# One group of square sums, an earlier modulation column and sooner expected landings in a planned layer kernel

## The chip, the cores and the metric

The kernel runs on one core of a Trainium2 chip, in one launch. The metric is the device time in microseconds of that core. A core has a tensor engine (TensorE, PE in the profile) that multiplies matrices out of SBUF into PSUM, a vector engine (VectorE, DVE), a scalar engine (ScalarE, ACT), a general engine (GpSimd, POOL) and a queue engine (SyncE, SP) that here issues nearly all DMA loads. Each engine takes its instructions strictly in the order in which the program gives them.

## The reference

One layer over 512 latent tokens and 256 context tokens of width 1024, in float32. The part that the change is about is the opening: the modulation from c, the normalisation of x, and the first projection.

```python
def rms_norm(x, w):
    y = xf * lax.rsqrt(jnp.mean(xf * xf, axis=-1, keepdims=True) + EPS)
    return (y * w.astype(jnp.float32)).astype(x.dtype)

def modulate(h, shift, scale):
    return h * (1 + scale) + shift
...
mod_x = jnp.split((jax.nn.silu(c) @ w_mod[l] + b_mod[l])[:, None, :], N_MOD, axis=-1)
mod_c = jnp.split((jax.nn.silu(c_ctx) @ w_mod[l] + b_mod[l])[None, None, :], N_MOD, axis=-1)
cq_x, ckv_x, kr_x, z_x, xbc_x, dt_x = in_split(
    modulate(rms_norm(x, mix_pre_norm[l]), mod_x[0], mod_x[1]) @ w_in[l])
```

After it come latent attention over 16 heads, a bidirectional state-space scan over 16 heads (whose output is multiplied by silu(z)), one output projection, a normalised residual, and a gated MLP of inner width 2816 with a convolution of width 3 on the gate.

## The kernel before

x lies transposed: 8 blocks of 128 features by 512 tokens. Wide products run as three passes of 32-bit reduced precision on split operands (a rounded part and the rest, made by ScalarE at L500 and VectorE at L501).

**Opening.** The 8 blocks of x are loaded first (L492), then small parameters, then the weights block by block. ScalarE squares each block (L611, in `token_scale`). VectorE adds squares (L613); the argument `firsts` names the blocks at which a new group of adds starts. When a group ends, four products with a column of ones (L619, two instructions each) add it over the features into one bank. With groups at 0, 2, 4 and 6 there are four adds and 16 products. Then VectorE takes mean and inverse root (L623, L522 to L531), four products (L537) spread the result as a row, and ScalarE copies it (L630).

The modulation of a block needs two dot products of silu(c) with columns k and 8+k of `w_mod`. For blocks 2, 4 and 6 (`ON_PE`) TensorE does them (`moddots`, L599: eight products for a column, 16 instructions); for the others VectorE does (`moddot`, L589), with c spread over all partitions by `spread` (L664, L666). `modulated` (L635 to L645) applies scale and shift. Then 12 products of 512 columns (`half_of_z`, L687) add block k to the first half of z. Blocks go in the order 0, 2, 1, 4, 3, 6, 5, 7. The second half of z and the later projections follow.

Filler products on zeros (L680, 128 x 128 times 128 x 256) stand in three lots whose sizes are `IDLE`. The first must come before the spread of c, the second after it, the third after the products of the square sums.

**The planner.** The order on each engine is not the order of the source. `plan` prices each instruction, builds the dependences, and `Graph.schedule` lists them by rank, forward and backward, over 24 rounds, together with the place of each buffer in SBUF; the round with the shortest planned time is kept. Loads marked `urgent` keep the order of the source. `pins` are added dependences between products: each pair of instructions in one stretch must precede all of another. The second column of block 2 is pinned behind the z products of block 0, its first behind L537; the columns of blocks 4 and 6 behind z products of blocks before theirs. Filler that has no pin ahead of it is put wherever the plan has TensorE idle.

A load is planned as: issue, a start of 650 ns, a transfer at 360 bytes per ns behind all loads planned before it in the queue, and then a wait of 910 ns plus 0.8 of its transfer before its readers may start. At most eight loads are planned in flight. The planner also models TensorE's rate: it halves the rate in a tick of 3413 ns when too little was streamed in the tick before.

Of the kernel before, what the change touches and what calls it, by code (L numbers as in the profile page):

```python
# [20 lines left out]
S = 512  # L21
CT = 256
T = S + CT
KD = D // P
# [57 lines left out]

ON_PE = 2, 4, 6
BLOCKS = 0, 2, 1, 4, 3, 6, 5, 7
IDLE = 22, 13, 13
PACE = 1.25


# [24 lines left out]
class Banks:  # L113
# [18 lines left out]
    def put(self, *aps):  # L132
        for ap in aps:
# [6 lines left out]
WAITS = {("Activation", "Activation"): 75, ("Activation", "DVE"): 142, ("Activation", "PE"): 271, ("Activation", "Pool"): 170,  # L140
         ("DVE", "Activation"): 128, ("DVE", "DVE"): 127, ("DVE", "PE"): 256, ("DVE", "Pool"): 155,
         ("PE", "Activation"): 197, ("PE", "DVE"): 196, ("PE", "Pool"): 224,
         ("Pool", "Activation"): 75, ("Pool", "DVE"): 74, ("Pool", "PE"): 149, ("Pool", "Pool"): 102}

AHEAD = 40000
DMA_START, DMA_WAIT, DMA_AHEAD, DMA_ALONE, RUN, FLYING = 650, 910, 3000, 0.8, 80, 8


def engine_of(x):
# [113 lines left out]
class Graph:  # L263
# [16 lines left out]
    def wait(self, i, j):  # L280
        if self.back:
            i, j = j, i
        return DMA_WAIT + DMA_ALONE * self.cost[i] if self.dma[i] else WAITS.get((self.eng[i], self.eng[j]), 0)

    def reversed(self):
        g = Graph.__new__(Graph)
# [25 lines left out]
    def schedule(self, rank, look=0.06):  # L312

        n = len(self.preds)
        left, ready = [len(p) for p in self.preds], [0.0] * n
        start, end = [0.0] * n, [0.0] * n
        later, now = {e: [] for e in ENGINES}, {e: [] for e in ENGINES}
        clock, order, queue = {e: 0.0 if self.back else BEGIN for e in ENGINES}, {e: [] for e in ENGINES}, 0.0
        ticks, held, port, flying = {}, 0, 0.0, []
        for i in range(n):  # L320
            if not left[i]:
                ready[i] = max(0.0, rank[i] - AHEAD) if i in self.opens else 0.0
                heapq.heappush(later[self.eng[i]], (ready[i], rank[i], i))

        def open_until(e, t):
            while later[e] and later[e][0][0] <= t:
                _, r, i = heapq.heappop(later[e])
                heapq.heappush(now[e], (r, i))

        for _ in range(n):  # L330
            while True:
                at = []
                for e in ENGINES:
                    open_until(e, clock[e])
                    if now[e] or later[e]:
                        at.append((clock[e] if now[e] else later[e][0][0], e))
                t, e = min(at, key=lambda v: v[0])
                open_until(e, t)
                r, i = heapq.heappop(now[e])
                sooner = [v for v in later[e] if v[1] < r and v[0] < t + (look if v[1] > r - 5000 else 0.8) * self.cost[i]]  # L340
                if not sooner:
                    break
                heapq.heappush(now[e], (r, i))
                clock[e] = min(sooner, key=lambda v: v[1])[0]
            order[e].append(i)
            if self.tables[i] not in (None, held):
                held, t = self.tables[i], t + TABLE
            if self.shared[i]:
                t = max(t, port)
                port = t + self.cost[i]  # L350
            if self.dma[i] and not self.back and len(flying) >= FLYING:
                t = max(t, flying[-FLYING])
            start[i] = t
            end[i] = t + self.cost[i] if self.back or e != "PE" else self.product(t, i, ticks)
            clock[e] = end[i] + (3 if e == "PE" else 0)
            if self.dma[i] and e != "SP":
                end[i], clock[e] = max(t + self.dma[i] + DMA_START + 600, queue) + self.cost[i], t + 60
                queue += self.cost[i]
            if e == "SP":
                end[i] = queue = max(t + self.dma[i] + DMA_START, queue) + self.cost[i]  # L360
                clock[e] = t + self.dma[i] if self.back else max(t + self.dma[i], queue - DMA_AHEAD)
            if self.dma[i]:
                flying.append(end[i] + DMA_WAIT + DMA_ALONE * self.cost[i])
            for j in self.succs[i]:
                ready[j] = max(ready[j], end[i] + self.wait(i, j))
                left[j] -= 1
                if not left[j]:
                    if j in self.opens:
                        ready[j] = max(ready[j], rank[j] - AHEAD)
                    heapq.heappush(later[self.eng[j]], (ready[j], rank[j], j))  # L370
        return max(end), order, start, end
# [97 lines left out]
def build(nc, tc, ctx, a, out, dbg=None, places=None):  # L469
    mm = nc.tensor.matmul  # L470
    act = nc.scalar.activation
    V, G = nc.vector, nc.gpsimd
# [10 lines left out]
    def t4(*shape, dt=F32):  # L483
        return sl.get(here(), shape or (P, 1024), dt)

    def t2(*shape, dt=F32):
        return sl.get(here(), shape or (P, 512), dt)
# [26 lines left out]
    def small(tag, w=1):  # L514
        cnt[0] += w
        return smalls[:, cnt[0] - w : cnt[0]]
# [17 lines left out]
    def rows_of(po, r, n):  # L534

        for i in range(n):
            mm(po[:, i * P : (i + 1) * P], lhsT=r[:, i : i + 1].to_broadcast([P, P]), rhs=ident, start=True, stop=True)  # L537
# [10 lines left out]
    xt = [t4(P, 2, S) for _ in range(4)]  # L548
# [17 lines left out]
    def R(name, j=0, n=1):  # L566
        o, w = PRM[name]
        return prm[:, o + j : o + j + n]
# [22 lines left out]
    def moddots(k, w0, w1, pm):  # L591

        for n, w in enumerate((w0, w1)):
            began = here()
            at = BLOCKS.index(k) - 3 + n
            o = products[BLOCKS[max(at, 0)]] if at > -2 else rows
            pins.extend(((o[0] + i, o[0] + i + 2), (began, began + KD)) for i in range(0, o[1] - o[0], 2))
            for r in range(KD):
                mm(pm[:, 2 * n : 2 * n + 2], lhsT=w[:, r * P : (r + 1) * P], rhs=cc[:, 2 * r : 2 * r + 2], start=r == 0,  # L599
                   stop=r == KD - 1)  # L600
        for n, md in enumerate((mod, modc)):
            V.tensor_tensor(out=md[:, k:16:8], in0=pm[:, n:4:2], in1=R("bmod", k, 9)[:, 0:9:8], op=ALU.add)

    def token_scale(blocks, n, firsts, kind):


        nt = n // P
        pS, began = pget(kind), here()
        for i, b in enumerate(blocks):
            sq = t2()  # L610
            act(sq if len(b.shape) == 2 else sq.rearrange("p (a b) -> p a b", a=2), b, AF.Square)  # L611
            if i not in firsts:
                firsts[j].tensor_tensor(out=part, in0=part, in1=sq, op=ALU.add)  # L613
            else:
                part, j = sq, i
            if i + 1 in firsts or i + 1 == len(blocks):
                for o in range(0, S, n):
                    for c in range(nt):
                        mm(pS[:, c : c + 1], lhsT=part[:, o + c * P : o + (c + 1) * P], rhs=ones[:, :1],  # L619
                           start=j == o == c == 0, stop=(i + 1 == len(blocks) and o + n == S and c == nt - 1))  # L620
        summed = began, here()
        ss = small(f"ss{nt}", nt)
        V.tensor_scalar(out=ss, in0=pS[:, :nt], scalar1=1.0 / D, scalar2=EPS, op0=ALU.mult, op1=ALU.add)  # L623
        pfree(pS)
        pr = pget(kind)
        r, began = rsqrt(ss, nt), here()
        rows_of(pr, r, nt)
        rows = began, here()
        rB = t2(P, n)
        act(rB, pr[:, :n], AF.Copy)  # L630
        return rB, pr, summed, rows
# [23 lines left out]
    act(cch, cc, AF.Tanh, scale=0.5)  # L655
    V.scalar_tensor_tensor(out=cc, in0=cch, scalar=1.0, in1=cc, op0=ALU.add, op1=ALU.mult)
    V.tensor_scalar(out=cc, in0=cc, scalar1=0.5, scalar2=None, op0=ALU.mult)
    rB, pr, summed, rows = token_scale([xt[k // 2][:, k % 2, :] for k in range(KD)], S, {0: V, 2: V, 4: V, 6: V}, "b")


    def spread(i, v):
# [14 lines left out]

    for i, n in enumerate(IDLE):
        began = here()
# [18 lines left out]
    kept, products, pmod = {}, {}, pget("m")  # L697
    hx.extend([None] * KD)
    for k in BLOCKS:
# [15 lines left out]
        began = here()  # L715
# [174 lines left out]
    pr = pget("b")  # L890
# [529 lines left out]
    rows = {}  # L1420
# [300 lines left out]
```

## Time and profile before

| what | us |
|---|---|
| median of 3 runs (lowest to highest) | 966.89 (965.46 to 972.02) |
| the profiled execution's own time | 967.49 |
| its span, first to last instruction | 965.7 |
| mean granted TensorE clock in it | 0.987 |
| DMA packets' bytes in it | 137.53 MB, 142 GB/s on average |

The profile is of one execution. A page names lines as L and a number, engines by the short names above, PEld for TensorE's weight loads. Rows of the windows view give a stretch of the span, then busy time and instruction counts of engines, the granted TensorE clock as a share of full speed, the mean busy share of the DMA engines, and GB/s. Rows of the chain view give start, length, and what the time is put down to, on the chain of work that ended last. Rows of the timeline give start, length, engine, line, operation, what it writes and reads, and in brackets how long the engine was idle before and what released it. Rows of the waits view give who waited for whom: total, times, longest.

### The profile page before, as it was taken

To read this page: it belongs to the slowest core of one execution; us is meant where nothing else is said; L and a number is where in the kernel's file an instruction comes from. 1 tells how busy PE (TensorE), PEld (TensorE's weight loads), DVE (VectorE), ACT (ScalarE), POOL (GpSimd) and SP (SyncE) were. 2 spreads that over 40 slices of the span, in tenths; PEclk is the share of its full clock that TensorE was granted. 3 is DMA by queue.
4 is the path that set the end of the run, shared out by engine and by line. 5 is a ranking of instruction groups with operands and counts; after the bars stand their busy time and mean duration, and the time that the engine had idled before them with its cause. 6 is when DMAs were issued, how large, how long until landed. Compare 5 with 4: busy or idle time off the path is not lost.

```text
span 965.7 us, 14674 instructions
## 1 busy us (share of the span) xinstructions
PE 944.0 (98%) x5118; PEld 805.6 (83%) x5118; DVE 763.3 (79%) x1452; ACT 525.7 (54%) x1024; POOL 236.5 (24%) x246
## 2 busy tenths in 40 slices
PE   9999999999999999999999999999999999999995
PEld 9888888888788888888988888988888888887784
DVE  5799868789979999987999967943556442799998
ACT  4364336635677787778886215732324322257782
POOL 0001000547768546734010100000011042230021
PEclk6999999999999999999999999999999999999998
DMA  9943111102331441545678764523255132346883
GB/s 345 338 162 107 31 52 66 50 12 83 94 79 50 102 116 40 135 106 132 180 236 290 266 212 172 207 80 131 69 186 190 58 106 90 123 143 199 257 277 127
DMA packets 54586, 137.53 MB, mean 142 GB/s; under 512 B 8032, under 2 KB 11120, under 8 KB 54512
## 3 DMA queue, kind: packets, MB, share of 16 engines
q1 hardware_dynamic: 53712, 134.92, 43.1%
q10 hardware_dynamic: 800, 1.68, 0.5%
q8 instruction: 40, 0.66, 0.3%
q14 instruction: 34, 0.28, 0.1%
HBM read 114.50 MB, written 6.34 MB: 125 GB/s over the span
## 4 chain that ended last, share of the span: by engine, by line
PE 81%; DVE 12%; DMA 3%; ACT 2%; issue 1%; POOL 0%; SPq 0%; DVEq 0%; ACTq 0%; POOLq 0%
PE banks L755 40%; PE banks L1319 7%; PE banks L1189 6%; PE banks L1551 5%; PE banks L687 5%; DVE block L501 5%; PE banks L1217 4%; PE banks L1205 4%; DVE block L1544 2%; PE banks L1023 1%; PE banks L599 1%; PE banks L1069 1%; PE banks L1124 1%; PE banks L1061 1%; DMA block<-in_wdn_dram 1%
## 5 line engine op out<-in xcount | busy, mean ns | idle before, releaser
L755 PE MATMUL banks<-block,block 128*128 128x512 f32 (+1 forms) x2132 | 450.6, 361 | 1.8 <-DVE block L1415 0.8
L755 PEld LDWEIGHTS banks<-block,block 128*128 128x128 f32 x2132 | 358.1, 188 | 63.3 <-issue 1.1
L500 ACT ACTIVATE block<-block 128x512 fp32r<-128x512 f32 (+4 forms) x340 | 216.2, 663 | 154.1 <-PE banks L755 28.0
L501 DVE TENSOR_TENSOR block<-block,block 128x512 fp32r<-128x512 f32 (+3 forms) x316 | 245.0, 810 | 33.9 <-PE banks L755 16.4
L1551 PE MATMUL banks<-block,block 128*128 128x512 f32 x462 | 108.7, 391 | 1.0 <-DVE block L501 0.8
L1551 PEld LDWEIGHTS banks<-block,block 128*128 128x128 f32 x462 | 86.0, 188 | 21.6 <-DVE block L501 3.2
L1189 PE MATMUL banks<-block,block 128*128 128x256 f32 (+1 forms) x384 | 93.5, 351 | 2.8 <-DMA block<-block 1.6
L501 DVE TENSOR_TENSOR block<-banks,block 128x256 fp32r<-128x256 f32 (+1 forms) x156 | 83.5, 555 | 10.6 <-ACT block L500 10.1
L1319 PE MATMUL banks<-block,block 128*128 128x512 f32 x384 | 89.3, 391 | 0.0
L1319 PEld LDWEIGHTS banks<-block,block 128*128 128x128 f32 x384 | 71.6, 188 | 14.6 <-DVE block L501 0.2
L500 ACT ACTIVATE block<-banks 128x256 fp32r<-128x256 f32 (+1 forms) x156 | 72.3, 495 | 15.1 <-PE banks L1205 10.0
L1189 PEld LDWEIGHTS banks<-block,block 128*128 128x128 f32 x384 | 59.5, 189 | 9.8 <-ACT block L1193 3.0
L1191 DVE TENSOR_REDUCE smalls<-banks 128x1 f32<-128x768 f32 x64 | 60.8, 950 | 8.1 <-PE banks L1189 6.4
L1217 PE MATMUL banks<-block,block 128*128 128x256 f32 x384 | 66.2, 294 | 0.2 <-ACT block L1193 0.2
L1193 ACT ACTIVATE block<-banks,smalls 128x768 f32<-128x768 f32 x64 | 57.6, 901 | 15.0 <-DVE smalls L1191 13.3
L1205 PE MATMUL banks<-cst,block 128*128 128x128 f32 x384 | 64.4, 273 | 0.5 <-DVE block L501 0.3
L589 DVE SCALAR_TENSOR_TENSOR block<-block,block 128x1024 f32<-128x1024 f32 x52 | 62.4, 1216 | 1.8 <-DMA block<-in_wmod_dram 1.8
L1446 ACT ACTIVATE block<-banks,prm 128x512 f32<-128x512 f32 x22 | 16.9, 775 | 84.7 <-PE banks L755 84.7
L785 DVE SCALAR_TENSOR_TENSOR block<-banks,cwh,block 128x510 f32<-128x510 f32 (+3 forms) x88 | 51.6, 622 | 11.7 <-ACT block L781 11.1
L1217 PEld LDWEIGHTS banks<-block,block 128*128 128x128 f32 x384 | 54.7, 189 | 3.5 <-ACT block L1193 0.4
L1460 POOL TENSOR_TENSOR block<-block 128x256 f32<-128x256 f32 x11 | 12.5, 1132 | 169.2 <-PE banks L755 69.6
L1205 PEld LDWEIGHTS banks<-cst,block 128*128 128x128 f32 x384 | 46.7, 141 | 7.6 <-DVE block L501 1.7
(230 smaller groups left out, 1120.5 us busy)
## 6 DMA issues: line engine op xcount, KB each, us to landing
block<-in_wdn_dram SPq DMA_DIRECT2D x99, 256.0 KB
block<-in_wmod_dram SPq DMA_DIRECT2D x48, 512.0 KB
block<-in_wup_dram SPq DMA_DIRECT2D x44, 512.0 KB
block<-block SPq DMA_DIRECT2D x32, 256.0 KB
block<-in_wout_dram SPq DMA_DIRECT2D x16, 512.0 KB
block<-in_wxbc_dram SPq DMA_DIRECT2D x12, 512.0 KB
block<-block SPq DMA_DIRECT2D x40, 128.0 KB
block<-in_wz_dram SPq DMA_DIRECT2D x16, 256.0 KB
```

Of the source, the lines that this page charges most:

```text
L500: act(hi, src, AF.Copy)
L501: (lo_eng or V).tensor_tensor(out=lo, in0=src, in1=hi, op=ALU.subtract)
L589: V.scalar_tensor_tensor(out=junk, in0=wt, scalar=0.5, in1=vec, op0=ALU.mult, op1=ALU.mult, accum_out=acc)
L755: mm(po, lhsT=wf(k, pt[0]), rhs=xf(k, pt[1]), start=(k == 0 and pt == parts[0]), stop=(k == nk - 1 and pt == parts[-1]))
L785: V.scalar_tensor_tensor(out=st[:, lo:hi], in0=pm[:, lo + d : hi + d], scalar=cwh[:, m * 5 + j : m * 5 + j + 1], in1=st[:, lo:hi], op0=ALU ...
L1189: mm(sc[:, o : o + n], lhsT=q_[:, x_, qi * P : (qi + 1) * P], rhs=kk[:, y_, :], start=part == 0, stop=part == 2)
L1191: V.reduce_max(nm, sc[:, :T], axis=AX.X, negate=True)
L1193: act(pe, sc[:, :T], AF.Exp, bias=nm, scale=1.0, accum_out=sum_)
L1205: nc.tensor.transpose((tx if c < NX else tc_)[:, o : o + P], pe[:, s_ : s_ + P], ident)
L1217: mm(po[:, half * 256 : half * 256 + 256], lhsT=vst(c), rhs=rhs, start=(part == 0 and c == 0), stop=(part == 1 and c == NKT - 1))
L1319: mm(po[i][:, nh * 512 : nh * 512 + 512], lhsT=l[lp][:, i * P : (i + 1) * P], rhs=w[wp][:, nh * 512 : nh * 512 + 512], start=(k == 0 and l ...
L1551: mm(po[i], lhsT=l[:, lp, i * P : (i + 1) * P], rhs=w[wp], start=first and q == 0 and n == 0, stop=q == PAIRS[-1] and n == 2, skip_group_c ...
```

## The change

Four edits, in the order of the diff. The three lots of filler grow from 22, 13, 13 to 22, 44, 24. The planner's landing time changes: a load's data is now there at the later of its own undisturbed landing (start, 1.8 of its transfer) and the planned end of the queue less 600 ns, plus 910 ns; loads issued by engines other than SP now also start no earlier in the queue than their own start. This enters the forward plan, the backward plan and the count of loads in flight, so all orders and buffer places may come out differently. The second modulation column of block 2 is pinned behind the row products (L537) and no longer behind block 0's z products. The squares of x form one group: seven adds on VectorE, then four products.

```diff
-IDLE = 22, 13, 13
+IDLE = 22, 44, 24
...
-DMA_START, DMA_WAIT, DMA_AHEAD, DMA_ALONE, RUN, FLYING = 650, 910, 3000, 0.8, 80, 8
+DMA_START, DMA_WAIT, DMA_AHEAD, DMA_ALONE, RUN, FLYING, DMA_FULL = 650, 910, 3000, 0.8, 80, 8, 600
...
-        return DMA_WAIT + DMA_ALONE * self.cost[i] if self.dma[i] else WAITS.get((self.eng[i], self.eng[j]), 0)
+        return DMA_WAIT if self.dma[i] else WAITS.get((self.eng[i], self.eng[j]), 0)
...
             if self.dma[i] and e != "SP":
-                end[i], clock[e] = max(t + self.dma[i] + DMA_START + 600, queue) + self.cost[i], t + 60
-                queue += self.cost[i]
+                began = t + self.dma[i] + DMA_START + 600
+                queue = max(began, queue) + self.cost[i]
+                end[i], clock[e] = max(began + (1 + DMA_ALONE) * self.cost[i], queue - DMA_FULL), t + 60
             if e == "SP":
-                end[i] = queue = max(t + self.dma[i] + DMA_START, queue) + self.cost[i]
+                began = t + self.dma[i] + DMA_START
+                queue = max(began, queue) + self.cost[i]
+                end[i] = max(began + (1 + DMA_ALONE) * self.cost[i], queue - DMA_FULL)
                 clock[e] = t + self.dma[i] if self.back else max(t + self.dma[i], queue - DMA_AHEAD)
             if self.dma[i]:
-                flying.append(end[i] + DMA_WAIT + DMA_ALONE * self.cost[i])
+                flying.append(end[i] + DMA_WAIT)
...
             at = BLOCKS.index(k) - 3 + n
-            o = products[BLOCKS[max(at, 0)]] if at > -2 else rows
+            o = products[BLOCKS[at]] if at >= 0 else rows
...
-    rB, pr, summed, rows = token_scale([xt[k // 2][:, k % 2, :] for k in range(KD)], S, {0: V, 2: V, 4: V, 6: V}, "b")
+    rB, pr, summed, rows = token_scale([xt[k // 2][:, k % 2, :] for k in range(KD)], S, {0: V}, "b")
```

## The prediction

> **What bounds the kernel now.** I read the page's head first, then the busy time by stretches of the span, then the chain that ended last through the opening, and last the VectorE and ScalarE timelines of the same microseconds.
>
> ```profile
> span 965.7 us, 14674 instructions
> PE 944.0 (98%) x5118; PEld 805.6 (83%) x5118; DVE 763.3 (79%) x1452; ACT 525.7 (54%) x1024; POOL 236.5 (24%) x246
> PE 81%; DVE 12%; DMA 3%; ACT 2%; issue 1%; POOL 0%; SPq 0%; DVEq 0%; ACTq 0%; POOLq 0%
> ...
> 0.00:25.00 25.00, 23.27 (x113) 22.43 (x114) 13.34 (x40) 10.98 (x19) 0.80 (x7) 0.68 0.94 346
> 25.00:50.00 25.00, 25.00 (x151) 22.14 (x150) 18.94 (x42) 10.98 (x20) 0.00 (x0) 0.98 0.91 341
> 250.00:275.00 25.00, 22.05 (x134) 18.74 (x133) 22.53 (x43) 18.76 (x47) 15.37 (x16) 1.00 0.38 96
> 950.00:965.70 15.70, 4.51 (x20) 3.38 (x19) 11.58 (x49) 2.10 (x6) 1.29 (x1) 0.75 0.36 134
> ```
>
> TensorE is busy for 944.0 of 965.7 us, and the chain lies on it for 81%. So time is won only where TensorE does nothing, does filler, or runs slowly. Idle time is 21.7 us in all: 1.7 in the first 25 us, 11.2 in the tail after 950, and 8.8 spread between (the largest piece 2.95, in the stretch from 250). In the row from 25 to 50 there is none: products fill every gap. A product stream that starts its useful work earlier therefore ends earlier, as long as data is there. The granted clock (third number from the right) is 0.68 only in the first stretch. The opening is where the change's named parts lie:
>
> ```profile
> 1.20:5.65 4.45, 4.41 (x20) 1.00 0.83 252
> 5.65:9.06 3.41, 2.92 (x27) 1.00 1.05 367
> 9.06:12.47 3.41, 3.41 (x17) 0.50 1.01 389
> 12.47:15.89 3.42, 3.42 (x18) 0.50 1.04 416
> 19.30:22.71 3.41, 3.41 (x17) 0.50 1.04 405
> 22.71:26.13 3.42, 3.42 (x10) 0.50 0.97 327
> 26.13:29.54 3.41, 3.41 (x27) 1.00 0.98 389
> ...
> 7.75 0.50 PE banks L664 x4
> 8.25 0.84 PE banks L619 x8
> 10.28 1.79 PE banks L619 x8
> 12.49 1.50 PE banks L619 x8
> 13.99 2.77 PE banks L680 x12
> 16.76 1.81 PE banks L537 x8
> 18.57 3.21 PE banks L599 x16
> 21.77 1.27 PE banks L680 x5
> 23.05 4.25 PE banks L687 x12
> 27.29 1.68 PE banks L599 x16
> 28.97 0.71 PE banks L680 x5
> 31.36 2.87 PE banks L687 x12
> ```
>
> The first seven rows (TensorE alone: stretch, busy, products, granted clock, DMA share, GB/s) show the clock at half from 9.06 to 26.13 us, five steps of 3.41. The rest is the chain: L664 the spread of c over partitions, L619 the sums of squares, L680 filler, L537 the row of scales, L599 a modulation column, L687 z products. At half clock twelve z products take 4.25 us against 2.87 later, a column 3.21 against 1.68, eight sum products 1.79 against 0.84. The first block's z products end at 27.29, and only then comes block 2's second column (27.29) and filler (28.97). At 29.68 the next column starts; this is my yardstick, T.
>
> **The change, part by part.**
>
> ```profile
> 8.21 2.60 ACT L611 ACTIVATE block<-block 128x512 f32<-128x512 f32 x4 [1.05 <-DMA block<-in_xt_dram]
> 13.80 0.63 ACT L500 ACTIVATE block<-block 128x512 fp32r<-128x512 f32 x1 [1.98 <-DMA block<-in_wz_dram]
> 10.84 0.69 DVE L613 TENSOR_TENSOR block<-block,block 128x512 f32<-128x512 f32 x1 [0.17 <-ACT block L611]
> 14.03 0.16 DVE L623 TENSOR_SCALAR smalls<-banks 128x4 f32<-128x4 f32 x1 [2.05 <-PE banks L619]
> 16.27 0.16 DVE L531 SCALAR_TENSOR_TENSOR smalls<-smalls 128x4 f32<-128x4 f32 x1
> 17.50 1.22 DVE L589 SCALAR_TENSOR_TENSOR block<-block,block 128x1024 f32<-128x1024 f32 x1
> 19.75 0.91 ACT L642 ACTIVATE block<-block,mod 128x256 fp32r<-128x256 f32 x2
> 29.01 0.16 DVE L602 TENSOR_TENSOR mod<-banks,prm 128x2 f32<-128x2 f32 x1 [5.22 <-PE banks L599]
> 8.14 0.33 SPq L492 DMA_DIRECT2D block<-in_wz_dram  x1
> SPq L492 <- PE banks L599: 11.4, 2, 6.6
> ```
>
> Squares in one group. VectorE gets 7 adds instead of 4, three more at 0.69. They chain behind ScalarE's squares, which come every 0.65 us (2.60 for 4) and end at 10.81; the last add ends at 10.84 + 0.11 + 0.69 = 11.64 instead of 11.53. So the extra adds hide behind the landing of x, and cost 0.1. TensorE loses 24 of 32 sum instructions. Only the last group's place matters: now 24 of them run after 8.25, at half clock, so the last ends at 13.99, 2.4 us after its operand. With 8 left, they end at 11.8 + 0.84 = 12.6 at full clock, or 11.8 + 1.79 = 13.6 at half. The mean and root on VectorE (14.03 to 16.43, so 2.4) end at 15.0 or 16.0, and the rows (L537) at 16.0 (1.0, half of about 2.0 with its start) or 18.0.
>
> Block 2's second column goes ahead of z. Its two columns may now run right after the rows: 2 x 1.68 = 3.4 at full clock, 2 x 3.21 = 6.4 at half. Their weights' last byte is number 4.68 MB of the loads (x 2.10, small ones 0.22, four columns of 0.524, one wz of 0.262). By the GB/s of the stretches above, with 1.12 MB before 5.65, that passes at about 14.8; the wz load (byte 3.63 MB, about 12.3) was usable 1.5 later, so the second column's weight is there at 16.3, ahead of its turn. What queues behind the columns on TensorE are block 0's z products; they need the block's modulation, which ends as now by two dots after the root and ScalarE's pass: now the second dot ends at 18.7 (17.50 + 1.22) and the first half of ScalarE's pair at about 20.2 (19.75 and half of 0.91). With the root at 15.0 instead of 16.4 that is 18.8. Columns end at 16.0 + 3.4 = 19.4, so they hold z back by 0.6 at full clock, and by much more at half. In return VectorE's wait of 5.22 us for block 2's column goes; what is late next there is the dot products of block 1. SP gains too: two loads waited 11.4 us for buffers these columns hold. POOL's queue is not touched.
>
> More filler: 22, 13, 13 becomes 22, 44, 24. At full clock a filler product costs 0.14 (0.71 for 5), at half 0.23 (2.77 for 12). It costs nothing while TensorE would wait: from the spread's end (about 7 us, when its products, 0.50 for 4, no longer alternate with sums) to the last add (11.6) there is room for some 30, and in the root's 2.4 us for 10 to 17. Without that cover each is paid in full. What it buys is the clock. In the stretch to 9.06 TensorE was busy for 2.92 of 3.41, mostly with one-column products, and the clock fell; in the stretch to 26.13 z products filled it and the clock rose. Twelve fillers in the stretch to 15.89 did not raise it. I read this as a gate that counts streamed columns per 3.41 us. Filler from 7 to 9 us then holds the clock past 9.06; two columns of two elements each (L599) drop it one step later, so z runs slowly once more.
>
> The Trainium skill, "TensorE: Matmul & The Clock Gate", part 1, says the clock halves only after an idle window of about 3.4 us and returns after a busy one. The step length agrees with the rows (five steps of 3.41), the condition does not: the clock fell after a window busy for 2.92 us. By the page's rule busy columns would hold the clock, and the sum would be that of the full-clock case below.
>
> Sooner landings. By the code's own constants a load in a full queue is now expected 600 ns plus 0.8 of its transfer earlier, 1.8 us for 512 KB at its 360 bytes per ns, 1.2 for 256 KB; an isolated load as before. The wz load issued at 8.14 was used at 13.80; the old constants put it at about 13.2, the new ones at 12.0. So in the first microseconds the new plan counts on a load 1.8 too early instead of 0.6, and TensorE may idle at the sums' turn by as much. Later the queue moves 400 GB/s against the planned 360, so the error shrinks and turns. Everything after is rearranged (each engine's order and the buffers), which no row prices. Bounds: the 8.8 us of idle time between the ends could shrink by a third (-3) or grow by three landings of 1.8 (+5). I take 0, nearest the rows: in the whole kernel only 1.6 us of TensorE's idle time is put down to a DMA, in one place, while ScalarE's waits for loads are mostly covered:
>
> ```profile
> PE banks L1189 <- DMA block<-block: 1.6, 1, 1.6
> ACT block L500 <- DMA block<-in_wup_dram: 11.7, 8, 5.4
> ```
>
> **Sum.** Full clock throughout: columns end 19.4, z 2.9, T = 22.3 or, with 0.4 of handovers, 22.7: gain 7.0. Half throughout: rows 18.0, columns 24.4, z 4.25, T = 28.9 with handovers: gain 0.8. Mixed (full up to the columns, z at half): 19.4 + 0.4 + 4.4 = 24.2: gain 5.5. I take the mixed case, 5.5. VectorE follows: it loses the 5.22 wait, so it can feed blocks 5 us sooner. The profiled execution took 967.49 us (span 965.7, 1.8 around it); 967.5 - 5.5 = 962.0. The median of the runs is 0.6 below that execution, 966.89, so I predict 961.5 for it.
>
> **Rivals.** (a) Full clock, and the middle's stalls shrink by up to 3: 966.9 - 7.0 - 3 = 956.9, alone without the stalls 959.9. For it: filler now covers every gap. Against: columns stream almost nothing. The Trainium skill's rule named above would give this one. (b) The clock stays at half, so the change does little: 966.1. For it: twelve fillers at half clock did not raise it, and sums that come later than planned leave TensorE idle in the stretch from 9.06. (c) Slower: filler in the way. If the clock is half between sums and rows, the root's 2.4 us hides ten fillers at 0.23; all 24 of the last lot cost 14 x 0.23 = 3.2 more on the path to the rows, against 0.8 won: 966.9 + 2.4 = 969.3. It decides from 14 fillers there on. (d) Late landings: the plan puts products ahead of loads that come up to 1.8 us later. Nine such stalls undo 5.5 and add 1%; for it speaks the 11.7 us that ScalarE waits for wup already, against it that TensorE's own row shows 1.6: 978.
>
> **How the numbers follow.** Mixed 0.45, with its own range 957 to 966 by the rearrangement's -3 to +5; (a) 0.2; (b) 0.15; (c) 0.12; (d) 0.08. A measurement of this kernel tells 1%, some 9.7 us, from no change. Faster than 957.2: half of (a) and a little of the mixed case, 0.14. Slower than 976.6: most of (d), 0.06. Within: 0.80. The range 955 to 970 leaves out the lower end of (a), the upper of (c), and (d).
>
> **What would show it.** Right: eight L619 products after the last add; both L599 columns before the first L687; VectorE's 5.22 wait gone; the clock at 1.00 past 9.06; the first L687 ending by 25. Wrong: a half clock past 23, fillers between L623 and L537 that end after the root, or new TensorE idle time put down to DMA after 100 us, which would undo the sum wherever the opening ends.

## The result, and the profile after

| | median us | lowest to highest (runs) |
|---|---|---|
| before | 966.57 | 964.63 to 972.02 (20) |
| changed | 972.67 | 966.07 to 977.69 (20) |

The ratio of the changed kernel's time to the time before is 1.0058, with a 95% interval of 1.0042 to 1.0073; here and below the ratio leaves disturbed executions out and the medians do not, which matters for `land_only_m` alone (975.07 us, and 974.68 without its two). The change makes the kernel 0.6% slower; 0.6% faster was predicted. The profiled execution of the changed kernel took 969.76 us, its span 968.0, so it is one of its quicker ones, 2.9 below the median; the profiled execution of the kernel before lies 0.9 above its own. So the medians are 6.1 us apart and the traces 2.3.

First the same stretches of both traces, for TensorE alone: the stretch, its length and the busy time in it, products, granted clock, DMA share, GB/s. The cuts lie at the yardstick T of the prediction (after block 0's z products and block 2's columns, with the z products that follow taken off), the last z product, the last product of the output projection, and the first of the final down projection. Before:

```profile
0.00:29.68 29.68, 27.95 (x143) 0.71 0.95 350
29.68:164.70 135.02, 135.02 (x716) 1.00 0.34 116
164.70:598.80 434.10, 427.71 (x2569) 1.00 0.43 131
598.80:834.00 235.20, 233.78 (x1178) 1.00 0.35 120
834.00:965.70 131.70, 119.51 (x520) 0.97 0.61 200
```

After:

```profile
0.00:24.10 24.10, 22.10 (x140) 0.93 0.94 348
24.10:161.80 137.70, 137.32 (x734) 1.00 0.36 124
161.80:597.60 435.80, 429.19 (x2571) 1.00 0.43 129
597.60:835.80 238.20, 234.93 (x1174) 0.99 0.34 120
835.80:968.00 132.20, 120.59 (x524) 0.98 0.63 205
```

The opening is 5.6 us shorter, as predicted (5.5). Each later stretch is longer: 2.7, 1.7, 3.0 and 0.5 us, 7.9 together, and the sum of all five is the 2.3 us by which the span grew. TensorE's idle time in these four (length less busy time) grew by 1.9 us net, so most of the loss stands as busy time. Its busy time in all is what it was (944.0 us before, 944.1 now), although the opening saves 5.9 of it. The timeline of TensorE in the changed kernel's opening:

```profile
7.49 3.20 PE L683 MATMUL banks<-block 128*128 128x256 f32 x25
11.45 1.02 PE L622 MATMUL banks<-ones,block 128*128 128x1 f32 x8 [0.76 <-DVE block L616]
12.33 2.87 PE L683 MATMUL banks<-block 128*128 128x256 f32 x22
15.04 1.11 PE L540 MATMUL banks<-cst,smalls 128*128 128x128 f32 x8
...
16.22 3.63 PE L602 MATMUL banks<-cc,block 128*128 128x2 f32 x32
19.71 5.50 PE L690 MATMUL banks<-block,block 128*128 128x512 f32 x16
```

Lines are three higher than before (L683 filler, L622 sums, L540 rows, L602 columns, L690 z). Eight sum products follow the last add, the rows come at 15.0 to 16.2, both columns precede the first z product, and z starts at 19.7 instead of 22.84. Block 0's z products end at 24.1, the mixed case's 24.2 nearly to the tenth. But the second trace of the same kernel (`after_again` below) shows another opening:

```profile
6.65 3.20 PE L683 MATMUL banks<-block 128*128 128x256 f32 x25
12.04 1.84 PE L622 MATMUL banks<-ones,block 128*128 128x1 f32 x8 [2.19 <-DVE block L616]
13.73 5.02 PE L683 MATMUL banks<-block 128*128 128x256 f32 x22
18.57 1.07 PE L540 MATMUL banks<-cst,smalls 128*128 128x128 f32 x8
...
19.72 4.73 PE L602 MATMUL banks<-cc,block 128*128 128x2 f32 x32
24.31 6.02 PE L690 MATMUL banks<-block,block 128*128 128x512 f32 x16
```

The microsecond from 11 to 12 in the windows view (stretch, busy time, products, granted clock, DMA share, GB/s), first trace, then second:

```profile
11.00:12.00 1.00, 0.55 (x6) 1.00 0.98 395
```

```profile
11.00:12.00 1.00, 0.00 (x0) 0.88 1.00 395
```

In the second, 25 fillers end at 9.85 and TensorE does nothing until 12.04, because the sums' operand comes later than the plan has it. A step of the clock gate falls into that gap, the clock is at half from 11.8, and now 22 fillers at 0.23 us stand between the sums and the rows: 5.02 us where the root needs 2.4. That is rival (c), filler in the way, and z starts at 24.3. Here z's first block ends at 29.2 (its 16 products end as the next column starts at 30.17; the four that follow are taken off as above), 0.5 us sooner than before. The first trace has a gap too, 0.76 us, and kept its clock through the sums; what decides between the two, the place of the step or the length of the gap, two traces cannot tell.

The last two places to see are filler in the z stream, and the start of the gated MLP. Timeline of the changed kernel:

```profile
44.65 3.33 PE L690 MATMUL banks<-block,block 128*128 128x512 f32 x14
47.83 0.52 PE L683 MATMUL banks<-block 128*128 128x256 f32 x3
48.41 1.00 PE L683 MATMUL banks<-block 128*128 128x256 f32 x7
49.25 3.59 PE L690 MATMUL banks<-block,block 128*128 128x512 f32 x15
...
54.90 2.47 PE L690 MATMUL banks<-block,block 128*128 128x512 f32 x10
...
600.02 0.87 PE L758 MATMUL banks<-block,block 128*128 128x256 f32 x4 [0.27 <-ACT block L1417]
603.89 5.10 PE L758 MATMUL banks<-block,block 128*128 128x256 f32 x28 [3.00 <-DVE block L1418]
```

Between 47.8 and 54.9 stand 19 fillers and 21 z products (some single ones are left out above). At the rate of the first row (14 in 3.33) or a little above it, the z products take 4.9 of the 7.1 us, so the fillers cost 2.2: most of the 2.7 us lost in that stretch. In the kernel before, z products alone stand there:

```profile
44.91 12.44 PE L687 MATMUL banks<-block,block 128*128 128x512 f32 x53
```

At the MLP's start TensorE waits 3.00 us for VectorE, and the windows view gives the clock as 0.83 from 600 to 610: it fell for a step right behind the wait. In the kernel before the same place reads:

```profile
600.71 0.71 PE L755 MATMUL banks<-block,block 128*128 128x256 f32 x4
602.26 3.60 PE L755 MATMUL banks<-block,block 128*128 128x256 f32 x28 [0.84 <-DVE block L1415]
```

28 products took 3.60 us there and take 5.10 now. No DMA ends either wait. But the long wait belongs to this execution and not to the new order as such. In the second trace, with the same order, it is 0.99 us, and the clock stays up:

```profile
605.65 2.18 PE L758 MATMUL banks<-block,block 128*128 128x256 f32 x16 [0.99 <-DVE block L1418]
```

In the first trace one operation of the root on VectorE, just ahead of L1418's operands, took 1.16 us, where the same step took 0.16 in the kernel before (first row); what held it is not shown, nor what made up the rest of the difference.

```profile
600.14 0.16 DVE L531 SCALAR_TENSOR_TENSOR smalls<-smalls 128x1 f32<-128x1 f32 x1
600.65 1.16 DVE L534 SCALAR_TENSOR_TENSOR smalls<-smalls 128x1 f32<-128x1 f32 x1
```

The five stretches of the second trace, cut at the same places:

```profile
0.00:29.20 29.20, 25.77 (x139) 0.77 0.86 323
29.20:167.00 137.80, 137.42 (x736) 1.00 0.35 117
167.00:602.10 435.10, 429.11 (x2571) 1.00 0.43 131
602.10:837.10 235.00, 233.74 (x1174) 1.00 0.34 119
837.10:970.50 133.40, 120.59 (x524) 0.98 0.63 203
```

Against the kernel before, its later stretches differ by +2.8, +1.0, -0.2 and +1.7 us, 5.3 together. So the z stream's loss and a part of the next stretch's stand in both traces, and the 3.0 us at the MLP in one only.

### The profile page after: what moved, and what is told of

Same layout as the page of the kernel before. It is cut to its first block, busy times and chain, and to the rows that moved or that the text cites. A ratio compares the mean times of both kernels' runs of the same rounds, so it can differ in the third digit from the quotient of the medians.

```text
span 968.0 us, 14745 instructions
## 1 busy us (share of the span) xinstructions
PE 944.1 (98%) x5136; PEld 803.9 (83%) x5136; DVE 763.6 (79%) x1455; ACT 525.4 (54%) x1024; POOL 237.2 (25%) x246
## 4 chain that ended last, share of the span: by engine, by line
PE 60%; DVE 15%; DMA 3%; issue 2%; ACT 2%; POOL 0%; SPq 0%; ACTq 0%; DVEq 0%; POOLq 0%
PE banks L758 32%; PE banks L1554 7%; PE banks L1192 6%; DVE block L504 5%; PE banks L1220 4%; PE banks L1208 3%; PE banks L1322 2%; PE banks L1127 2%; PE banks L1026 1%; DVE block L1547 1%; DVE block L1047 1%; DVE block L592 1%; DVE smalls L1194 1%; ACT block L503 1%; PE banks L1072 1%
## 5 line engine op out<-in xcount | busy, mean ns | idle before, releaser
L503 ACT ACTIVATE block<-block 128x512 fp32r<-128x512 f32 (+4 forms) x340 | 216.7, 664 | 187.9 <-DMA block<-in_wup_dram 39.5
L1554 PE MATMUL banks<-block,block 128*128 128x512 f32 x462 | 109.1, 391 | 1.4 <-ACT block L503 1.3
L1322 PE MATMUL banks<-block,block 128*128 128x512 f32 x384 | 89.3, 390 | 0.0
L1220 PE MATMUL banks<-block,block 128*128 128x256 f32 x384 | 68.4, 294 | 0.1
L788 DVE SCALAR_TENSOR_TENSOR block<-banks,cwh,block 128x511 f32<-128x511 f32 (+3 forms) x88 | 51.4, 620 | 11.8 <-ACT block L784 11.1
L690 PE MATMUL banks<-block,block 128*128 128x512 f32 x192 | 51.1, 406 | 0.0
```

What stands on the lines that cost most here:

```text
L503: act(hi, src, AF.Copy)
L788: V.scalar_tensor_tensor(out=st[:, lo:hi], in0=pm[:, lo + d : hi + d], scalar=cwh[:, m * 5 + j : m * 5 + j + 1], in1=st[:, lo:hi], op0=ALU ...
L1220: mm(po[:, half * 256 : half * 256 + 256], lhsT=vst(c), rhs=rhs, start=(part == 0 and c == 0), stop=(part == 1 and c == NKT - 1))
L1322: mm(po[i][:, nh * 512 : nh * 512 + 512], lhsT=l[lp][:, i * P : (i + 1) * P], rhs=w[wp][:, nh * 512 : nh * 512 + 512], start=(k == 0 and l ...
L1554: mm(po[i], lhsT=l[:, lp, i * P : (i + 1) * P], rhs=w[wp], start=first and q == 0 and n == 0, stop=q == PAIRS[-1] and n == 2, skip_group_c ...
```

## The experiments

All medians below are set beside runs of the kernel before on the same chip.

| label | median us | lowest to highest (runs) | before | ratio, 95% interval |
|---|---|---|---|---|
| after_again | 973.56 | 965.54 to 979.89 (12) | 967.55 | 1.0058, 1.0030 to 1.0086 |
| open_only | 967.34 | 964.92 to 971.65 (12) | 967.55 | 1.0001, 0.9978 to 1.0024 |
| land_only | 977.22 | 975.12 to 982.27 (6) | 967.55 | 1.0098, 1.0067 to 1.0129 |
| graft_open | 965.31 | 962.44 to 968.51 (12) | 966.67 | 0.9972, 0.9948 to 0.9996 |
| graft_rest | 983.44 | 980.79 to 983.87 (6) | 966.67 | 1.0148, 1.0113 to 1.0184 |
| null_b1 | 973.23 | 971.89 to 979.20 (12) | 966.67 | 1.0065, 1.0043 to 1.0087 |
| null_b2 | 971.64 | 966.61 to 975.67 (12) | 966.67 | 1.0044, 1.0020 to 1.0067 |
| graft_more | 963.39 | 962.52 to 967.00 (12) | 966.88 | 0.9972, 0.9958 to 0.9987 |
| surg_pin | 969.04 | 964.10 to 973.94 (12) | 966.88 | 1.0019, 0.9999 to 1.0039 |
| surg_group | 966.72 | 964.93 to 972.30 (12) | 966.88 | 1.0010, 0.9989 to 1.0030 |
| null_a1 | 969.89 | 964.89 to 973.26 (11) | 966.88 | 1.0031, 1.0008 to 1.0054 |
| null_a2 | 974.56 | 967.87 to 976.61 (12) | 966.82 | 1.0047, 1.0019 to 1.0074 |
| open_only_m | 968.82 | 967.72 to 975.28 (12) | 966.82 | 1.0014, 0.9991 to 1.0038 |
| land_only_m | 975.07 | 971.18 to 987.25 (12) | 966.82 | 1.0073, 1.0044 to 1.0102 |

### The halves of the change

The first batch runs the changed kernel again and each half alone.

> The changed kernel once more, for a second trace. Theory A (the loss is in the plan of the later work, the same in every execution): the opening's first twelve z products end near 25 us as in the first trace, and the output projection's end again costs some 4 us more than before. Theory B (the clock gate's steps fall differently from run to run, and that makes the spread of 966 to 978 us): an execution with a mean granted clock of 0.987 to 0.989 takes 974 to 978 us, one of 0.993 to 0.996 takes 966 to 971 us, and a trace of the slow kind shows three or four more steps of 3.41 us at half clock than the first trace, in the opening or after the output projection.

Both theories hold in part. Of the first 20 executions of the changed kernel, the eight with a mean clock of 0.987 to 0.989 took 974.75 to 977.69 us, the ten with 0.993 to 0.996 took 966.07 to 972.50. The second trace (0.990) has four steps at half clock in the opening (11.8 to 18.6, 22.0 to 28.8) where the first has one there (20.9 to 24.3) and one at the MLP's start. So the spread goes with the clock: 0.006 less of it in the mean, over some 970 us, is 5.8 us, and the two lots lie 6.5 apart on average.

```diff
 # open_only: the kernel before, with
-IDLE = 22, 13, 13
+IDLE = 22, 44, 24
-            o = products[BLOCKS[max(at, 0)]] if at > -2 else rows
+            o = products[BLOCKS[at]] if at >= 0 else rows
-    ... S, {0: V, 2: V, 4: V, 6: V}, "b")
+    ... S, {0: V}, "b")
 # land_only: the changed kernel, with these three undone
```

> The three opening edits (one group of squares, the earlier pin, more filler) with the old landing times in the planner. Theory A (the sooner landings spoil the plan of the later work): 961 to 963 us, the opening's gain of 5.5 kept. Theory C (any new plan of the later work comes out some microseconds better or worse, whatever the landing times): the opening is as in the changed kernel, but the total lies anywhere from 961 to 973 us, with idle TensorE time in other places than before. Theory B: the spread between executions is as wide as the changed kernel's (over 8 us).

> The planner's sooner landings alone, with the opening as before. Theory A: 972 to 978 us, as the loss of 8 to 11 us stands without the opening's gain, with ScalarE's waits for loads longer and TensorE idle behind them. Theory C: 963 to 973 us, and the loss not tied to waits for loads. Theory B: the spread is that of the kernel before (8 us or less), since its opening is unchanged.

Theory A got the second right (977.2) and the first wrong: with the old landings and the new opening the time is 967.3 and not 961.5. Its trace has the new opening (z from 20.7, half clock for one step only in it), and loses what it won later: the last product of the output projection starts at 601.1 there, at 598.8 before, at 597.6 in the changed kernel's first trace. So the sooner landings can't be the whole cause.

### Grafts: one kernel's opening on the other's rest

The planner's result is an order for each engine and a place for each buffer. Here it is stored instead of computed, so that a part of it can be exchanged.

```diff
 def program(arrays, dbg_shapes=None, **kw):
-    try:
-        trace(arrays, None, dbg_shapes, **kw)
-    except Traced as t:
-        tiles, hints, ins = t.args
-    return trace(arrays, plan(ins, tiles, hints, UNITS), dbg_shapes, **kw)
+    places, order = json.loads(zlib.decompress(base64.b85decode(ORDER)))
+    return trace(arrays, (0, [(o, bool(n)) for o, n in places], order), dbg_shapes, **kw)
 # graft_open: the changed kernel, IDLE = 22, 44, 5; 188 instructions of its order, then the order before
 # graft_rest: the kernel before, IDLE = 22, 13, 8; 171 instructions of its order, then the changed order
```

> The changed kernel's opening (everything up to block 0's first z products and block 2's two columns, in the changed kernel's order, with the 71 fillers that stood there) followed by the order and the buffer places of the kernel before; the 19 fillers that came later are left out. If the opening's gain is real and the loss lies in the new plan of the rest: 961 to 963 us in executions where the clock holds through the sums, 966 to 967 where it does not, so a median near 964 against 967.5. Theory D (the opening's gain is lost later whatever the order, because a later stage waits for other engines): 967 to 968, with new idle time after 200 us.

> The mirror: the opening of the kernel before, then the changed kernel's order and buffer places (without the five fillers after block 0's z products). If the loss lies in the new plan of the rest: 973 to 977 us, 6 to 9 above the kernel before. Theory D: 967 to 969.

Both come out as the theory that blames the rest has it, the second by more than it said: 983.4, partly at the seam (its trace has the clock at half from 28.4 to 45.5). The opening's gain reaches the end when the rest keeps its order: 965.3, against 966.7. The executions fall into two lots, five at 962.4 to 963.6 and seven at 964.9 to 968.5, with mean clocks of 0.994 to 0.996 and of 0.990 to 0.993. The trace is of the second lot; its TensorE idles 1.13 us ahead of the sums, and the clock is at half from 13.4, right behind them. That the first lot holds the clock there is not seen. The next kernel closes the gap ahead of the sums.

```diff
 # graft_more: graft_open, with IDLE = 22, 44, 16, and on TensorE
-  22 fillers, spread, 25 fillers, sums, 22 fillers, rows, 2 fillers, both columns, z
+  22 fillers, spread, 36 fillers, sums, 22 fillers, rows, 2 fillers, both columns, z
```

> As the graft of the changed opening onto the old order, with 36 fillers instead of 25 between the spread of c and the sums, so that TensorE does not fall idle while the last squares are added. If the gap of 0.8 to 2.2 us ahead of the sums is what lets the clock fall in some executions: the clock stays at 1.00 from its first rise to the columns (about 19 us) in every execution, the median falls from 965.3 to 962 to 963.5 us and the spread to 5 us or less. If the clock falls for another reason (the columns, or the phase alone): 965 to 966 with the same spread of 6 us, and 1 us more where the extra fillers stand in the way of the sums.

It has the lowest median, 963.39 us, inside the expected range, and eight of twelve executions lie within 1.5 us (962.5 to 964.0); the others reach 967.0. As a ratio to the kernel before it is the 0.9972 of `graft_open` again, so a gain over that graft is not clear of noise. Its TensorE timeline, and its stretches with the cuts as above:

```profile
7.38 4.53 PE L683 MATMUL banks<-block 128*128 128x256 f32 x36
11.74 0.95 PE L622 MATMUL banks<-ones,block 128*128 128x1 f32 x8
12.55 2.87 PE L683 MATMUL banks<-block 128*128 128x256 f32 x22
15.27 1.08 PE L540 MATMUL banks<-cst,smalls 128*128 128x128 f32 x8
...
19.91 4.58 PE L690 MATMUL banks<-block,block 128*128 128x512 f32 x12
24.33 1.84 PE L602 MATMUL banks<-cc,block 128*128 128x2 f32 x16
```

```profile
0.00:24.30 24.30, 23.06 (x150) 0.93 0.94 351
24.30:159.50 135.20, 135.20 (x717) 1.00 0.36 130
159.50:593.50 434.00, 427.64 (x2569) 1.00 0.43 131
593.50:828.60 235.10, 233.71 (x1177) 1.00 0.34 120
828.60:961.40 132.80, 119.51 (x520) 0.97 0.59 198
```

No wait stands in front of the sums any more. The opening is 5.4 us shorter than before, the next three stretches differ from those before by 0.2 at most, the last is 1.1 longer. This is the opening's price by itself, one trace against one; between the medians it is 3.5 us, by the ratio 2.7.

### New plans of the rest, with nothing else changed

If any new plan costs time, it should show with a constant that has nothing to do with the change. The opening's order stays the same in these.

```diff
 # null_b1 (the kernel before), null_a1 (the changed one), open_only_m, land_only_m
-UNITS, EDGE, MARGIN = 212, 168, 2500
+UNITS, EDGE, MARGIN = 212, 168, 2400
 # null_b2 (the kernel before), null_a2 (the changed one)
-AHEAD = 40000
+AHEAD = 41000
```

> The kernel before with a planner constant changed that has nothing to do with landings (the margin by which a buffer must be free ahead of its use, 2500 to 2400 ns); the opening's order stays, the later order and most buffer places come out anew. Theory A (the sooner landings spoil the rest): 966 to 969 us, as the landings are the old ones. Theory C (any new plan of the rest is some microseconds worse than this one, which is a favourable one): 970 to 977 us.

> Another new plan of the rest with the old landings (the earliest start of a load ahead of its need, 40000 to 41000 ns). Theory A: 966 to 969 us. Theory C: 970 to 977 us, and idle TensorE time in other places than with the margin of 2400.

Both take 5 to 7 us more than before, with the old landings and the old opening. Theory A is out as the whole cause: beside these two, the kernel before has a favourable plan of its rest. The stretch from the last z product to the end of the output projection, 434.10 before, is 442.00 in `null_b1`, with the same products, 4.2 us more idle time (10.6 against 6.4) and 3.7 more busy time, in which lies a step at half clock at 264 us:

```profile
163.10:605.10 442.00, 431.37 (x2570) 1.00 0.43 129
```

> The changed kernel with the margin at 2400 instead of 2500 ns: its opening's order stays, the later order and the buffer places come out anew with the sooner landings. If the loss is that of any new plan: 968 to 976 us, as far from the changed kernel's 973 as the two new plans with old landings were from each other. If the sooner landings spoil each plan beyond that: 975 to 980.

> The changed kernel with the loads' earliest start at 41000 instead of 40000 ns: its opening's order stays, the rest comes out anew with the sooner landings. Cost of any new plan: 968 to 974 us, like the first such kernel's 969.9. Sooner landings worse in themselves: 974 to 980.

> The three opening edits with the old landings, and the margin at 2400 instead of 2500 ns: a second plan of the rest with old landings. Cost of any new plan alone: 967 to 973 us, as the opening gains 1.5 to 3.5 and the rest loses 4 to 7. Sooner landings the main cause: at most 966.

> The sooner landings with the opening edits undone, and the margin at 2400 instead of 2500 ns: a second plan to set beside 977. Cost of any new plan alone: 968 to 974 us, so that 977 was one poor plan. Sooner landings worse in themselves: 975 to 980 again.

The difference of each median from the kernel before beside it (`land_only_m` by 974.68):

| plan of the rest | opening as before | opening edits in |
|---|---|---|
| new, old landings | +6.6, +5.0 | -0.2, +2.0 |
| new, sooner landings | +9.7, +7.9 | +6.1, +3.0, +7.7 |

Down the columns, plans with the sooner landings are 3.0 us slower on average (8.8 against 5.8) and 4.7 (5.6 against 0.9). But with the same margin of 2400 the two kinds differ by 1.3 (7.9 against 6.6) and 1.0 (3.0 against 2.0) only, and plans of one kind differ among themselves by up to 4.7. Whether the sooner landings spoil the plan beyond what any new plan does stays open. From left to right the opening edits gain 4.9 and 3.1.

### Two edits of the opening by themselves

These keep the order and places of the kernel before and move one thing, so no new plan is in the way.

```diff
 # surg_pin: on TensorE
-  block 2's first column, 5 fillers, z of block 0, block 2's second column
+  block 2's first column, 5 fillers, block 2's second column, z of block 0
 # surg_group: IDLE = 22, 13, 13 and firsts = {0: V}; seven adds, four products where the last group's stood
```

> The order and buffer places of the kernel before, with one thing moved: block 2's second column (eight products) ahead of block 0's z products. The prediction's step: VectorE's wait of 5.22 us for this column goes, but z starts later by the column at half clock (3.2 us), as clock and sums are as before: TensorE's sum changes by the column's 1.5 us more, so 966 to 969 us, no gain by itself. Rival: VectorE's 5 us were what the later blocks waited for, and the total falls to 961 to 964.

> The order and buffer places of the kernel before, with the squares in one group (seven adds, four products at the place of the last group). The prediction's step at half clock: the sums end 0.4 to 1.4 us earlier, total 965.5 to 967. Rival: the gaps that the missing products leave let the clock stay down longer and the total rises to 968 to 970.

Neither gains by itself. With the column moved, z starts at 23.6 and VectorE's waits for columns are still 4.6 us in two pieces; 969.0 lies at the upper end of the step's range, and the rival (961 to 964) is out. With one group, 966.7, within its range. In the one trace of `surg_group` z starts at 20.1 without any more filler, with the clock at half from 11.0 to 18.0 only, and that execution took 965.35 us. I read the two runs so, which they do not show by themselves: at half clock the moved column costs TensorE what it saves VectorE, and it pays only with filler that holds the clock, as in the grafts. Filler alone was not tried.

## Why the prediction was wrong, step by step

**The opening was right in its mechanism; its size is that of some executions.** T came at 24.1 in the first trace, predicted 24.2, and 5.4 us earlier than before in the kernel that holds the clock. The last add, the eight products and the rows at 16 are as written, and VectorE's wait of 5.22 us is gone with the first trace's opening. But two things in the size were luck. The T of before, 29.68, is that of an execution with five steps at half clock. `null_b1`, whose opening has the same order, has three (8.4 to 18.7), and the column that stands for T starts 2.9 us sooner there:

```profile
21.50 3.02 PE L687 MATMUL banks<-block,block 128*128 128x512 f32 x12
...
26.74 1.84 PE L599 MATMUL banks<-cc,block 128*128 128x2 f32 x16
```

And the 4.25 us for twelve z products "at half clock" is a row whose last 1.2 us ran at full clock; in the changed kernel the first 1.2 us did, so it fitted. With the old rest kept, the changed kernel's opening gains 1.4 us between the medians (`graft_open`) and 3.5 with the gap filled (`graft_more`), by the ratio 2.7 in both, where the sum took 5.5.

**It does not hold in each execution.** The prediction gave the mixed case and rival (c) as alternatives; the kernel has both. The plan counts on the sums too early, as the prediction said ("TensorE may idle at the sums' turn by as much"), but it priced this at nothing. The gap was 0.76 us in one trace and 2.19 in the other, and the clock fell in it or not.

**The step that failed is the rearrangement, taken at 0 with bounds of -3 and +5.** Two new plans of the rest, with old landings and the old opening, cost 6.6 and 5.0 us. The changed kernel itself is 6.1 above the kernel before, and its opening on the old rest 1.4 below: 7.5 us for the rest, between medians and with the 19 later fillers, which the graft leaves out, in it (its later stretches cost 7.9 in the first trace and 5.3 in the second). It was mis-sized in two ways. The bounds were drawn around the present plan's idle time as if a new plan could fall on either side of it; each of the two redrawn with unrelated constants was worse. Why the present plan is the better one stays open. And only waits were counted: 19 fillers that the plan put into the z stream cost 2.2 us there. The prediction said that filler without cover is paid in full, and then its sum priced none of the 42 more.

**Rival (d) named the wrong wait.** Nine late landings on TensorE were its price. TensorE's waits for DMA in the changed kernel come to 0.4 us, against 1.6 before. ScalarE's wait for wup, which spoke for the rival, did grow, from 11.7 to 39.5 us, but no row shows it handed on to TensorE. The waits of TensorE that are new in both traces end on VectorE and ScalarE: 1.6 and 1.5 us at L945, 1.1 and 1.1 at L1026.

## What to carry to other kernels

Where one planner orders the whole kernel, a local edit is two changes: the edit, and a new draw of everything behind it. Measure the spread of such draws with an unrelated constant before pricing the edit, and keep the part of the order that was good if it can be kept. Filler that bridges a wait should reach to the real end of that wait, not the planned one: with eleven more of them ahead of the sums the wait there was gone, and eight of twelve executions lay within 1.5 us. And a gain read from one trace of before is only as good as that execution is typical: here the same opening came 2.9 us sooner in another trace.

## What the runs showed of the hardware

In the traces of before and of the changed kernel the stretches at half clock ahead of the tail are 3.41 us long or whole numbers of it, but where the steps fall against the kernel's start differs from execution to execution: the half clock began at 9.06 us in the trace before, at 20.9 and at 11.8 in the two traces of the changed kernel. The Trainium skill, "TensorE: Matmul & The Clock Gate", part 1, says that the window runs freely and does not start with the kernel, and that the number of slow products varies with it; these runs agree, and here it goes with two lots of executions of one kernel some 6.5 us apart (970 and 976 us on average). A wait of 3.00 us in the middle was followed by a step at half clock, and so cost 1.5 us more than its length: 28 products took 5.10 us instead of 3.60. Behind the wait of 0.99 us at the same place in the second trace the clock stayed at 1.00.
